# Down projection of an encoder trunk: one product of the next visit ahead of the last two of this one

## The chip, the cores and the metric

The kernel runs on one core of a Trainium2 chip, in one launch. The metric is the time of one execution on the device in microseconds (us). Three runs of the kernel before took 2561.51 to 2565.45 us, with a median of 2564.89 us. The engines are PE (TensorE: matrix products), DVE (VectorE), ACT (ScalarE), POOL (GpSimd), and SP, which only issues transfers here. Each engine works through its own list of instructions in order and waits at an instruction until its inputs are there.

## The reference

Two layers on 1024 tokens of width 1024, all in float32. The first mixes the tokens by attention and retention, the second by gated linear attention (GLA); each ends with a gated MLP whose gate goes through a convolution of width 3.

```python
for layer in range(2):
    if layer % 2 == 0:
        h = rmsnorm(x, mix_norm_even)
        x = x + concat(mla(...), retention(...)) @ w_out_even
    else:
        h = rmsnorm(x, mix_norm_odd)
        x = x + gla(...) @ w_out_odd
    h = rmsnorm(x, ffn_norm[layer])
    gate, val = split(h @ w_up[layer])            # 2 x 2816 columns
    gate = conv3(gate, conv_w[layer]) + conv_b[layer]
    x = x + (silu(gate) * val) @ w_down[layer]    # the down projection

# inside gla, for each of 4 heads (128 wide) and 2 directions:
log_a = log_sigmoid(ga @ w_gate + b_gate) / 16
b = cumsum(log_a)                                 # within a chunk
qc, kc = q * exp(b - b_mid), k * exp(b_mid - b)
out = mask(qc @ kc.T) @ v + (q * exp(b)) @ state
g = rmsnorm(out_fwd + out_bwd, out_norm) * silu(gr)
```

## The kernel before

Products in float32 are made of three passes: both operands are split into a high and a low part (`split`, L327: a cast on ACT at L329 and a subtraction on DVE or POOL at L330), and `mm3` (L348, its matmuls at L351) multiplies high by high, high by low and low by high.

The instructions are recorded in the order of the Python code, and a scheduler then orders each engine's list by its own estimate of who is ready. The order is fixed when the program is built. `act_set` (L145) asks for one instruction, the preload of a set of function tables on ACT (L146), to stay where the program put it.

**Tables on ACT.** A function such as Silu, Exp or Ln needs its set of tables to be the active one; where it is not, the built program has an `ACT_TABLE_LOAD` in front of the instruction. The set that is preloaded at L146, `natural_log_exp_and_others`, has Exp and Ln both. Without it, Exp and Ln each bring a set of their own. Silu (L1291, in the up projection) has another. The order of the kernel before has six loads: three at L146, two at L1291 and one at L257.

**Up projection.** `ffn` (L1133) makes 22 blocks of 128 columns of the gated product, each ended by `gated_mid` (L1279: convolution on DVE, Silu at L1291). `Mid` (L1298) writes the products to memory, the first 16 also as the differences that the down projection needs.

**Down projection** (`Down`, L1340). The first 16 blocks (`PAIRED`) are multiplied by a scheme of seven products in place of eight for a 2 x 2 block of the output. `VISITS` (L31) lists nine visits: the pair of output rows `m`, the first group of four blocks `g`, and one or two groups. The products of a visit are numbered 0 to 6 (A11, S2, A12, S3, S1, A22, S4, by the weight that they take) and add up in four banks: 0 and 2 in the first, 1 in the second, 3 and 5 in the third, 4 and 6 in the fourth. After each product DVE adds the bank to the output tile (L1437; the very first product of a pair is copied by ACT, L1435). So product 5 starts when DVE has added product 3, and between them on PE lies product 4 alone, and product 6 the same after 4.

Weights go through `weights` (L1380: four transfers a visit on SP, and two sums on POOL, L1389 and L1390), called when the first part of the visit ahead is due; `part` (L1394) splits one weight five products ahead of its use (`LEAD`), and after products 0 and 2 it asks POOL for the two other sums (L1406, L1408), which are written over a weight that has just been split or to a page of their own. The operands of a group come back from memory by `operands` (L1361). Six plain blocks follow (from L1487).

In the first layer `run` (L1449) asks for the preload of the Ln and Exp tables at L1453, since the norm and the GLA section that follow use them. In GLA the lines at stake are: the gates' Abs, Exp and Ln (L998 to L1000), the decays' Exp (L988), the output gates (L608, L609 and L611: Exp, Ln and Exp), the root of the norms by Ln and Exp (L359 to L361: Ln, Exp, Square), which DVE finishes at L363, and the copies L1021 and L1040. On PE they feed L854 (transposes), L1034 (states), L1104 (outputs, whose squares ACT sums at L1107) and L1119 (their transposes, after ACT has scaled them at L1113), woven between matmuls at L351 of the projections.

Of the kernel before, what the change touches and what calls it, by code (L numbers as in the profile page):

```python
# [10 lines left out]
F32 = mybir.dt.float32  # L11
# [3 lines left out]
ALU = mybir.AluOpType  # L15
AX = mybir.AxisListType

P = 128
# [4 lines left out]
H2 = 512  # L23
# [6 lines left out]
PAIRED, LEAD = 16, 5  # L30
VISITS = [(0, 0, 1), (2, 0, 2), (4, 0, 2), (6, 0, 2), (0, 1, 2), (2, 2, 2), (4, 2, 2), (6, 2, 2), (0, 3, 1)]  # L31
# [37 lines left out]
class Encoder:  # L69
# [1063 lines left out]
    def ffn(self, layer, h, ws, scale, h_gain, xs, gain=None, ahead=None):  # L1133
# [3 lines left out]
        nc = self.nc  # L1137
        mid = Mid(self)
        with ExitStack() as stack:
# [7 lines left out]
            with self.room("right", pp=2, wf=2):  # L1147
# [3 lines left out]
                r = scale()  # L1151
# [16 lines left out]
            with self.room("right", wf=6, sw=2):  # L1168
# [3 lines left out]
                for i, (g, then) in enumerate(zip(steps, steps[1:] + [None]), 3):  # L1172
                    next(g)
                    if then:
                        next(then)
                    else:
                        for p in range(1, 5):
                            down.operands(0, p)
                        down.begin()
                    for _ in g:  # L1180
                        pass
                    if i == PAIRED + 1:
# [157 lines left out]
class Down:  # L1340
# [8 lines left out]
    def __init__(self, e, layer, mid):  # L1349
        self.e, self.nc, self.mid = e, e.nc, mid  # L1350
        self.w = e.io["ffn_w_down"][layer].rearrange("(k p) f -> p k f", p=P)
        self.b, self.parts, self.raw, self.loads = {}, {}, {}, 0

    def stage(self, src):

# [24 lines left out]
    def weights(self, v):  # L1380

        e, nc, (m, g, n) = self.e, self.nc, VISITS[v]
        wg, wv = (e.page([P, 2, 2 * n, P], F32, "rb" if v % 2 else "raw") for _ in range(2))
        for x, c in ((wg, m), (wv, m + 1)):
            src = self.w[:, 4 * g:4 * (g + n), blk(c)].rearrange("p (j two) f -> p two j f", two=2)
            for i in range(2):
                nc.sync.dma_start(out=x[:, i], in_=src[:, i])
        s1, s4 = (e.page([P, 2 * n, P], tag="hx") for _ in range(2))
        nc.gpsimd.tensor_tensor(s1, wv[:, 0], wv[:, 1], ALU.add)  # L1389
        nc.gpsimd.tensor_tensor(wv[:, 0], wg[:, 0], wv[:, 0], ALU.subtract)  # L1390
        self.raw[v] = {self.A11: wg[:, 0], self.S2: wg[:, 0], self.A12: wg[:, 1], self.S3: wv[:, 0], self.S1: s1,
                       self.A22: wv[:, 1], self.S4: s4}

    def part(self, s):  # L1394

        if s >= 7 * len(VISITS):
            return
        e, nc, (v, p) = self.e, self.nc, divmod(s, 7)
# [5 lines left out]
        self.parts[s] = t  # L1404
# [10 lines left out]
    def product(self, s, ps, first):  # L1415
        t, (_, g, n) = self.parts.pop(s), VISITS[s // 7]
        bs = [b for i in range(n) for b in self.b[g + i, s % 7]]
        for j, b in enumerate(bs):
            self.e.mm3(ps, (t[:, 0, j], t[:, 1, j]), b, first and j == 0, j == 2 * n - 1, not first)

    def visit(self, v):
        e, nc, (m, g, n) = self.e, self.nc, VISITS[v]
        first, last = m not in self.u, g + n == PAIRED // 4
        if first:
            for i in range(2):
                for hf in range(2):
                    nc.sync.dma_start(out=self.x[m + i][hf], in_=self.xs[2 * (m + i) + hf])
            self.u[m] = e.page([P, H2], tag="hx")
        (c11, c12), (c21, c22), u = *self.x[m:m + 2], self.u[m]
        b1, b2, b3, b4 = (e.bank() for _ in range(4))  # L1430
        for p, (ps, x) in enumerate(((b1, u), (b2, u), (b1, c11), (b3, c22), (b4, c22), (b3, c21), (b4, c12))):
            s = 7 * v + p
            self.product(s, ps, p in (0, 1, 3, 4))
            if first and p == 0:
                nc.scalar.copy(x, ps)  # L1435
            else:
                nc.vector.tensor_tensor(x, ps, x, ALU.add)  # L1437
            self.part(s + LEAD)

            then = {0: 1, 3: 2, 4: 3}.get(v)  # L1440
            if then:
                self.operands(then, p)
            if v in (7, 8) and p in (1, 3, 4):
                self.rest({1: 0, 3: 1, 4: 2}[p] + 3 * (v - 7), {1: 2, 3: 3, 4: 1}[p])
        if last:
            for x in (c21, c12, c22):
                nc.gpsimd.tensor_tensor(x, x, u, ALU.add)

    def run(self, xs, gain, ahead, stack, ends):  # L1449
        e, nc, io = self.e, self.nc, self.e.io  # L1450
        self.xs, self.u = xs, {}
        if gain is not None:
            e.act_set(LN_EXP)  # L1453
            e.x_rooms()
# [248 lines left out]
```

## Time and profile before

| | |
|---|---|
| median of three runs | 2564.89 us (2561.51 to 2565.45) |
| the profiled execution | 2564.21 us |
| its span on the core | 2562.0 us |
| mean granted clock of PE over the span | 0.996 |
| down projection of layer 0 | 1166.1 to 1334.0 us |
| down projection of layer 1 | 2314.3 to 2484.1 us |
| GLA section | from about 1450 to 1808 us |

The prediction's rows come from one execution. A row of the timeline gives the start of an instruction (or of several alike, as x12), its duration, engine, line, operation, what it writes and reads, the form, and in brackets how long the engine had been idle before it and who released it. A clock of 1.00 is 2.4 GHz on PE, and 0.50 is 1.2 GHz.

### The profile page before, as it was taken

To read this page: it belongs to the slowest core of one execution; us is meant where nothing else is said; L and a number is where in the kernel's file an instruction comes from. 1 tells how busy PE (TensorE), PEld (TensorE's weight loads), DVE (VectorE), ACT (ScalarE), POOL (GpSimd) and SP (SyncE) were. 2 spreads that over 40 slices of the span, in tenths; PEclk is the share of its full clock that TensorE was granted. 3 is DMA by queue.
4 is the path that set the end of the run, shared out by engine and by line. 5 is a ranking of instruction groups with operands and counts; after the bars stand their busy time and mean duration, and the time that the engine had idled before them with its cause. 6 is when DMAs were issued, how large, how long until landed. Compare 5 with 4: busy or idle time off the path is not lost.

```text
span 2562.0 us, 33330 instructions
## 1 busy us (share of the span) xinstructions
PE 2501.4 (98%) x12584; PEld 2091.9 (82%) x12584; DVE 1811.6 (71%) x2855; ACT 1209.5 (47%) x2229; POOL 273.0 (11%) x286
## 2 busy tenths in 40 slices
PE   8999999999999999999999999999999999998999
PEld 8989877777888888887788898897788888886787
DVE  6545887878578877778767545648578777778762
ACT  5233767778444333334434445657443333334432
POOL 0000033443000000003230000000000000003330
PEclk9999999999999999999999999999999999999999
DMA  6111100003622332437524211223732332437523
GB/s 195 40 46 42 51 26 5 14 18 124 206 91 87 107 114 94 131 102 246 165 68 144 58 54 44 77 66 112 254 92 89 107 99 97 131 105 247 160 64 121
DMA packets 305813, 262.20 MB, mean 102 GB/s; under 512 B 15916, under 2 KB 240277, under 8 KB 305653
## 3 DMA queue, kind: packets, MB, share of 16 engines
q1 hardware_dynamic: 301045, 251.69, 31.1%
q10 hardware_dynamic: 4608, 8.39, 0.9%
q8 instruction: 99, 1.62, 0.3%
q14 instruction: 61, 0.50, 0.1%
HBM read 189.52 MB, written 70.52 MB: 101 GB/s over the span
## 4 chain that ended last, share of the span: by engine, by line
PE 67%; DVE 17%; DMA 6%; ACT 6%; issue 3%; POOL 1%; SPq 0%; DVEq 0%; ACTq 0%; POOLq 0%
PE mm L351 57%; DMA raw<-in_ffn_w_up 3%; DVE pg L1290 2%; ACT w L329 2%; DVE w L330 2%; DVE hx L1260 1%; PE mr L1104 1%; PE mr L351 1%; DMA pg<-d 1%; PE mr L1542 1%; DVE pg L1294 1%; DVE hx L330 1%; PE mr L1597 1%; PE mr L1544 1%; DVE h L330 1%
## 5 line engine op out<-in xcount | busy, mean ns | idle before, releaser
L351 PE MATMUL mm<-hx,w 128*128 128x512 f32 (+1 forms) x3408 | 828.9, 394 | 7.1 <-DVE w L330 2.5
L351 PEld LDWEIGHTS mm<-hx,w 128*128 128x128 f32 (+1 forms) x3408 | 635.9, 188 | 145.0 <-DVE w L330 3.4
L351 PE MATMUL mm<-h,w 128*128 128x512 f32 x1800 | 433.7, 394 | 14.4 <-DVE xt L1437 6.1
L351 PEld LDWEIGHTS mm<-h,w 128*128 128x128 f32 x1800 | 339.0, 190 | 90.2 <-DVE xt L1437 5.3
L329 ACT CAST w<-raw 128x1024 fp32r<-128x1024 f32 (+3 forms) x307 | 244.5, 802 | 354.6 <-PE mm L351 207.2
L330 DVE TENSOR_TENSOR w<-raw,w 128x1024 fp32r<-128x1024 f32 (+3 forms) x257 | 262.3, 1024 | 176.1 <-ACT w L329 159.8
L351 PE MATMUL mm<-w,hx 128*128 128x256 f32 (+1 forms) x2304 | 364.4, 306 | 2.4 <-POOL w L330 1.8
L351 PE MATMUL mm<-h,wf 128*128 128x512 f32 x1368 | 329.5, 390 | 2.6 <-DVE hx L1260 2.5
L351 PEld LDWEIGHTS mm<-w,hx 128*128 128x128 f32 x2304 | 308.0, 192 | 21.4 <-POOL w L330 2.8
L351 PEld LDWEIGHTS mm<-h,wf 128*128 128x128 f32 x1368 | 256.4, 188 | 58.1 <-DVE hx L1260 4.1
L1389 POOL TENSOR_TENSOR hx<-raw 128x512 f32<-128x512 f32 (+1 forms) x10 | 12.4, 1238 | 1545.4 <-ACT pg L1285 962.5
L329 ACT CAST wf<-raw 128x1024 fp32r<-128x1024 f32 x78 | 82.1, 1053 | 177.1 <-DVE raw L1246 133.1
L1260 DVE TENSOR_TENSOR hx<-mm,hx 128x512 f32<-128x512 f32 x190 | 130.2, 685 | 46.6 <-PE mm L351 46.6
L351 PE MATMUL mm<-hx,wf 128*128 128x512 f32 x552 | 132.4, 390 | 0.0
L351 PEld LDWEIGHTS mm<-hx,wf 128*128 128x128 f32 x552 | 103.4, 188 | 22.5 <-DVE hx L1260 1.1
L330 DVE TENSOR_TENSOR wf<-raw,wf 128x1024 fp32r<-128x1024 f32 x78 | 95.5, 1224 | 17.9 <-ACT wf L329 17.9
L351 PE MATMUL mm<-hr,hr 128*128 128x512 f32 x336 | 104.2, 404 | 1.4 <-ACT hf L1626 1.4
L1291 ACT ACTIVATE pg<-pg 128x1024 f32<-128x1024 f32 x44 | 46.7, 1062 | 122.7 <-DVE pg L1290 122.7
L1290 DVE SCALAR_TENSOR_TENSOR pg<-mm,c,pg 128x512 f32<-128x512 f32 (+1 forms) x100 | 73.7, 748 | 29.2 <-ACT pg L1285 29.2
L351 PE MATMUL mm<-hf,w 128*128 128x512 f32 x384 | 88.9, 392 | 0.0
L351 PEld LDWEIGHTS mm<-hf,w 128*128 128x128 f32 x384 | 72.2, 188 | 16.0
L330 POOL TENSOR_TENSOR w<-raw,w 128x512 fp32r<-128x512 f32 (+1 forms) x50 | 69.6, 1391 | 138.6 <-ACT w L329 94.0
(385 smaller groups left out, 3393.2 us busy)
## 6 DMA issues: line engine op xcount, KB each, us to landing
raw<-in_ffn_w_up SPq DMA_DIRECT2D x88, 512.0 KB
pg<-d SPq DMA_DIRECT2D x52, 512.0 KB
d<-tt SPq DMA_DIRECT2D x64, 256.0 KB
d<-pg SPq DMA_DIRECT2D x55, 256.0 KB
raw<-in_ffn_w_down SPq DMA_DIRECT2D x32, 384.0 KB
raw<-in_w_in_odd SPq DMA_DIRECT2D x24, 512.0 KB
raw<-in_w_out_even SPq DMA_DIRECT2D x16, 512.0 KB
st<-d SPq DMA_DIRECT2D x16, 512.0 KB
```

Source lines behind the costliest of these rows:

```text
L329: self.nc.scalar.copy(hi, src)
L330: return (rest or self.nc.vector).tensor_tensor(lo, src, hi.bitcast(F32), ALU.subtract)
L351: mm = lambda w, x, start, stop: self.nc.tensor.matmul(out, lhsT=w, rhs=x, start=start, stop=stop, skip_group_check=more)
L1104: nc.tensor.matmul(ps, lhsT=w[:, blk(t % 4)], rhs=x, start=n == 0, stop=n == len(terms) - 1)
L1260: add = lambda out, x, y: nc.vector.tensor_tensor(out, x, y, ALU.add)
L1290: nc.vector.scalar_tensor_tensor(dst, g[hf][:, src], cw(tap), dst, ALU.mult, ALU.add)
L1291: nc.scalar.activation(cv, cv, AF.Silu)
L1294: nc.vector.tensor_tensor(cv[:, sl], cv[:, sl], v[hf], ALU.mult)
L1389: nc.gpsimd.tensor_tensor(s1, wv[:, 0], wv[:, 1], ALU.add)
L1542: nc.tensor.matmul(ps[:, :192], lhsT=e.cq[k][hf][:, blk(t % 4)], rhs=w1[:, k], start=k == 0, stop=k == 2)
L1544: nc.tensor.matmul(ps[:, 256:], lhsT=e.ckv[k][hf][:, blk(t % 4)], rhs=w2[:, k], start=k == 0, stop=k == 1)
L1597: nc.tensor.matmul(ps, lhsT=qs.tok(0, t)[0], rhs=ks.hi[0][hf], start=True, stop=True)
```

## The change

The products of all visits are put in one list, `seq`: after products 1 to 4 of a visit comes product 0 of the next, and then products 5 and 6 of the first. `slot(k)` does the k-th of the list, `part(k)` its weight, five places ahead. The transfers of a visit's weights move to a place after the last split of the visit two before it, and its first two sums and the S2 sum (L1398 of the new kernel, on a page of its own) to a place after the split of the S3 weight of the visit before. S4 takes the page of A12. Product 0 of the first visit is recorded ahead of the rest of the last block of the up projection, and `begin` ahead of the operands of products 1 to 4.

```diff
                     else:
+                        down.begin()
                         for p in range(1, 5):
                             down.operands(0, p)
-                        down.begin()
+                        down.slot(0)
...
+        n = len(VISITS)
+        self.seq = [(0, 0)] + [x for v in range(n) for x in [(v, p) for p in range(1, 5)] + [(v + 1, 0), (v, 5), (v, 6)] if x[0] < n]
...
-        s1, s4 = (e.page([P, 2 * n, P], tag="hx") for _ in range(2))
+
+    def sums(self, v):
+        e, nc, (wg, wv) = self.e, self.nc, self.raw[v]
+        s1, s2 = (e.page([P, 2 * VISITS[v][2], P], tag="hx") for _ in range(2))
         nc.gpsimd.tensor_tensor(s1, wv[:, 0], wv[:, 1], ALU.add)
+        nc.gpsimd.tensor_tensor(s2, s1, wg[:, 0], ALU.subtract)
         nc.gpsimd.tensor_tensor(wv[:, 0], wg[:, 0], wv[:, 0], ALU.subtract)
-        self.raw[v] = {self.A11: wg[:, 0], self.S2: wg[:, 0], self.A12: wg[:, 1], self.S3: wv[:, 0], self.S1: s1,
-                       self.A22: wv[:, 1], self.S4: s4}
+        self.raw[v] = {self.A11: wg[:, 0], self.S2: s2, self.A12: wg[:, 1], self.S3: wv[:, 0], self.S1: s1,
+                       self.A22: wv[:, 1], self.S4: wg[:, 1]}
...
-        if not p and v + 1 < len(VISITS):
-            self.weights(v + 1)
...
-        if p == self.A11:
-            nc.gpsimd.tensor_tensor(r[p], r[self.S1], r[p], ALU.subtract)
         if p == self.A12:
             nc.gpsimd.tensor_tensor(r[self.S4], r[p], r[self.S2], ALU.subtract)
+        if p == self.S3 and v + 1 < len(VISITS):
+            self.sums(v + 1)
+        if p == self.S4 and v + 2 < len(VISITS):
+            self.weights(v + 2)
...
     def begin(self):
         self.weights(0)
-        for s in range(LEAD):
-            self.part(s)
+        self.weights(1)
+        self.sums(0)
+        for k in range(LEAD):
+            self.part(k)
...
+    def slot(self, k):
+        e, nc, (v, p) = self.e, self.nc, self.seq[k]
+        m, g, n = VISITS[v]
+        if not p:
+            self.ps[v] = [e.bank() for _ in range(4)]
...
+        if p == 1 and v < 4:
             for i in range(2):
                 for hf in range(2):
                     nc.sync.dma_start(out=self.x[m + i][hf], in_=self.xs[2 * (m + i) + hf])
...
+        self.part(k + LEAD)
...
     def run(self, xs, gain, ahead, stack, ends):
...
-        for v in range(len(VISITS)):
-            self.visit(v)
+        for k in range(1, len(self.seq)):
+            self.slot(k)
```

What the scheduler makes of it stands in the order of the built programs. First PE, at the end of a visit in the middle of layer 0's down projection, before (mm_11263 is the fourth bank, with product 4; mm_11262 the third, with product 5):

```order
L351 MATMUL mm_11263<-h_11083,w_11252 128x512
L351 MATMUL mm_11263<-h_11082,w_11252 128x512
L351 MATMUL mm_11262<-h_10939,w_11277 128x512
L351 MATMUL mm_11262<-h_10940,w_11277 128x512
...
L351 MATMUL mm_11262<-h_11098,w_11277 128x512
L351 MATMUL mm_11263<-hx_10945,w_11293 128x512
...
```

and of the changed kernel (mm_11222 and mm_11221 are the fourth and third banks, mm_11352 the first bank of the next visit):

```order
L351 MATMUL mm_11222<-h_11079,w_11258 128x512
L351 MATMUL mm_11222<-h_11078,w_11258 128x512
L351 MATMUL mm_11352<-hx_10775,w_11274 128x512
L351 MATMUL mm_11352<-hx_10776,w_11274 128x512
...
L351 MATMUL mm_11352<-hx_10919,w_11274 128x512
L351 MATMUL mm_11221<-h_10965,w_11294 128x512
L351 MATMUL mm_11221<-h_10966,w_11294 128x512
...
L351 MATMUL mm_11221<-h_11120,w_11294 128x512
L351 MATMUL mm_11222<-hx_10971,w_11310 128x512
```

Twelve matmuls of the next visit's product 0 now stand between products 4 and 5.

Second ACT, where layer 0's up projection ends, before (pg is the last block, L1291 its Silu, L146 the preload of the Ln and Exp tables):

```order
L329 CAST w_11013<-hx_10869 128x256
L329 CAST w_11039<-rb_10872 128x512
L329 CAST hx_10947<-pg_10943 128x512
L1291 ACTIVATE pg_10925<-pg_10925 128x1024
L146 ACT_TABLE_LOAD
L1435 COPY hx_10981<-mm_10982 128x512
```

and of the changed kernel, where the Silu stands at L1292 and the convolution's start at L1286:

```order
L1286 ACTIVATE pg_10951<-hx_10719,c_70 128x512
L146 ACT_TABLE_LOAD
L329 CAST w_11030<-raw_10834 128x256
L329 CAST w_11056<-hx_10865 128x512
L329 CAST w_11072<-rb_10840 128x512
L329 CAST w_11100<-rb_10841 128x512
L1292 ACT_TABLE_LOAD
L1292 ACTIVATE pg_10951<-pg_10951 128x1024
```

The preload stood behind the last Silu and now stands ahead of it, and the Silu has a load of its own. In the whole order of ACT the loads go from 6 to 95. Of the 89 more, one is this Silu's, and 88 stand from the norm after this down projection to the norm of the next MLP, in front of Ln (L359, L609, L1000) and of Exp (L360, L608, L611, L988, L999): 8 in the two norms, and 16, 18, 18 and 28 in the four heads of GLA.

Third ACT, in the part of GLA where head 1 starts (hf is an output gate, hr a gate of the decay), before:

```order
L608 ACTIVATE hf_14056<-hf_14056 128x512
L609 ACTIVATE hf_14056<-hf_14056 128x512
L998 ACTIVATE hr_14086<-mr_14085,c_70 128x512
L999 ACTIVATE hr_14086<-hr_14086 128x512
L611 ACTIVATE hf_14056<-hf_14056 128x512
L1000 ACTIVATE hr_14086<-hr_14086 128x512
L998 ACTIVATE hr_14102<-mr_14101,c_70 128x512
L999 ACTIVATE hr_14102<-hr_14102 128x512
L1000 ACTIVATE hr_14102<-hr_14102 128x512
```

and of the changed kernel:

```order
L608 ACTIVATE hf_14056<-hf_14056 128x512
L609 ACT_TABLE_LOAD
L609 ACTIVATE hf_14056<-hf_14056 128x512
L998 ACTIVATE hr_14086<-mr_14085,c_70 128x512
L999 ACT_TABLE_LOAD
L999 ACTIVATE hr_14086<-hr_14086 128x512
L611 ACTIVATE hf_14056<-hf_14056 128x512
L1000 ACT_TABLE_LOAD
L1000 ACTIVATE hr_14086<-hr_14086 128x512
L998 ACTIVATE hr_14102<-mr_14101,c_70 128x512
L999 ACT_TABLE_LOAD
L999 ACTIVATE hr_14102<-hr_14102 128x512
```

The activations stand in the same order as before, and between them are loads, ten from L609 here to the copy L1021 that ends this part (four of the ten in the rows shown).

## Rows read from the trace of the kernel before

**Rows 1.** The page's first part: busy time and share of the span by engine

```profile
PE 2501.4 (98%) x12584; PEld 2091.9 (82%) x12584; DVE 1811.6 (71%) x2855; ACT 1209.5 (47%) x2229; POOL 273.0 (11%) x286
```

**Rows 2.** Windows: layer 0's down projection, and its start; last columns clock, DMA share, GB/s

```profile
core 0: us, PE busy (x) PEld busy (x) DVE busy (x) ACT busy (x) POOL busy (x), PEclk, DMA share, GB/s
1166.00:1334.00 168.00, 158.84 (x679) 128.71 (x678) 124.22 (x164) 69.69 (x106) 59.11 (x40) 0.98 0.50 162
1170.00:1210.00 40.00, 35.65 (x146) 27.94 (x145) 35.74 (x47) 20.94 (x33) 13.50 (x8) 0.96 0.89 290
```

**Rows 3.** Waits in the two down projections: total us, times, longest

```profile
PE mm L351 <- DVE xa L1437: 4.8, 3, 2.3
PE mm L351 <- DVE w L330: 4.4, 4, 2.2
...
PE mm L351 <- DVE xt L1437: 6.1, 4, 2.2
```

**Rows 4.** Timeline of PE: start us, us, ..., [idle before, releaser]

```profile
1224.62 2.88 PE L351 MATMUL mm<-h,w 128*128 128x512 f32 x12
...
1237.58 3.02 PE L351 MATMUL mm<-h,w 128*128 128x512 f32 x12 [1.92 <-DVE xa L1437]
...
1259.21 4.54 PE L351 MATMUL mm<-h,w 128*128 128x512 f32 x12 [2.29 <-DVE xa L1437]
...
2386.23 4.60 PE L351 MATMUL mm<-h,w 128*128 128x512 f32 x12 [1.93 <-DVE xt L1437]
...
2409.31 4.39 PE L351 MATMUL mm<-h,w 128*128 128x512 f32 x12 [2.15 <-DVE xt L1437]
```

**Rows 5.** Timeline of DVE ahead of that wait

```profile
1257.25 1.21 DVE L330 TENSOR_TENSOR h<-pg,h 128x1024 fp32r<-128x1024 f32 x1
1258.38 0.68 DVE L1437 TENSOR_TENSOR xa<-mm,xa 128x512 f32<-128x512 f32 x1
```

**Rows 6.** Window of one slow stretch of PE's clock

```profile
1260.27:1263.68 3.41, 3.41 (x10) 2.63 (x9) 2.86 (x4) 1.04 (x1) 0.00 (x0) 0.50 0.79 242
```

**Rows 7.** Timeline of ACT at the last Silu of layer 0

```profile
1172.23 1.06 ACT L1291 ACTIVATE pg<-pg 128x1024 f32<-128x1024 f32 x1 [0.50 <-DVE pg L1290]
1173.31 1.28 ACT L146 ACT_TABLE_LOAD   x1
1174.60 0.59 ACT L1435 COPY hx<-mm 128x512 f32<-128x512 f32 x1
```

**Rows 8.** Window of the GLA section

```profile
1450.00:1808.00 358.00, 352.56 (x2054) 306.22 (x2053) 218.30 (x362) 212.58 (x455) 0.00 (x0) 1.00 0.24 74
```

**Rows 9.** Instruction groups of ACT there: busy us, mean ns, idle before, releaser

```profile
L988 ACT ACTIVATE hr<-hr 128x512 f32<-128x512 f32 (+1 forms) x96 | 49.8, 554 | 14.8 <-DVE hr L1010 14.5
...
L1107 ACT ACTIVATE hr<-mr 128x256 f32<-128x256 f32 x32 | 11.9, 378 | 35.7 <-PE mr L1104 35.7
```

**Rows 10.** Timeline of ACT, start of GLA's head 1

```profile
1546.22 0.63 ACT L609 ACTIVATE hf<-hf 128x512 f32<-128x512 f32 x1
...
1553.12 0.61 ACT L988 ACTIVATE hr<-hr 128x512 f32<-128x512 f32 x1
...
1557.71 0.21 ACT L988 ACTIVATE sr<-hr 128x4 f32<-128x4 f32 x1 [1.56 <-DVE hr L1004]
1557.83 0.57 ACT L1021 COPY hr<-mr 128x512 f32<-128x512 f32 x1
```

**Rows 11.** Timeline of all engines there: DVE's and PE's rows

```profile
1554.60 0.69 DVE L1018 TENSOR_TENSOR hr<-hr,hf 128x512 f32<-128x512 f32 x1
...
1555.34 0.66 PE L854 MATMUL mr<-c,hr 128*128 128x128 f32 x4 [0.57 <-DVE hr L1018]
...
1558.45 0.91 PE L1034 MATMUL mr<-hf,hr 128*128 128x256 f32 x3
```

**Rows 12.** Timeline of all engines at an output norm of head 0

```profile
1541.32 1.57 ACT L1113 ACTIVATE hr<-mr,sr 128x256 f32<-128x256 f32 x4 [0.46 <-DVE sr L363]
1543.71 1.03 PE L1119 MATMUL mr<-c,hr 128*128 128x128 f32 x8
```

More of the change, by code (lines that the diff above doesn't have):

```diff
@@ L1351, in __init__ @@
         self.w = e.io["ffn_w_down"][layer].rearrange("(k p) f -> p k f", p=P)
-        self.b, self.parts, self.raw, self.loads = {}, {}, {}, 0
+        self.b, self.parts, self.raw, self.loads, self.u, self.ps = {}, {}, {}, 0, {}, {}
+        n = len(VISITS)
+        self.seq = [(0, 0)] + [x for v in range(n) for x in [(v, p) for p in range(1, 5)] + [(v + 1, 0), (v, 5), (v, 6)] if x[0] < n]
     def stage(self, src):
@@ L1382, in weights @@
         e, nc, (m, g, n) = self.e, self.nc, VISITS[v]
-        wg, wv = (e.page([P, 2, 2 * n, P], F32, "rb" if v % 2 else "raw") for _ in range(2))
-        for x, c in ((wg, m), (wv, m + 1)):
+        self.raw[v] = [e.page([P, 2, 2 * n, P], F32, "rb" if v % 2 else "raw") for _ in range(2)]
+        for x, c in zip(self.raw[v], (m, m + 1)):
             src = self.w[:, 4 * g:4 * (g + n), blk(c)].rearrange("p (j two) f -> p two j f", two=2)
@@ L1387, in weights, with part @@
                 nc.sync.dma_start(out=x[:, i], in_=src[:, i])
-        s1, s4 = (e.page([P, 2 * n, P], tag="hx") for _ in range(2))
+    def sums(self, v):
+        e, nc, (wg, wv) = self.e, self.nc, self.raw[v]
+        s1, s2 = (e.page([P, 2 * VISITS[v][2], P], tag="hx") for _ in range(2))
         nc.gpsimd.tensor_tensor(s1, wv[:, 0], wv[:, 1], ALU.add)
+        nc.gpsimd.tensor_tensor(s2, s1, wg[:, 0], ALU.subtract)
         nc.gpsimd.tensor_tensor(wv[:, 0], wg[:, 0], wv[:, 0], ALU.subtract)
-        self.raw[v] = {self.A11: wg[:, 0], self.S2: wg[:, 0], self.A12: wg[:, 1], self.S3: wv[:, 0], self.S1: s1,
-                       self.A22: wv[:, 1], self.S4: s4}
-    def part(self, s):
-        if s >= 7 * len(VISITS):
+        self.raw[v] = {self.A11: wg[:, 0], self.S2: s2, self.A12: wg[:, 1], self.S3: wv[:, 0], self.S1: s1,
+                       self.A22: wv[:, 1], self.S4: wg[:, 1]}
+    def part(self, k):
+        if k >= len(self.seq):
             return
-        e, nc, (v, p) = self.e, self.nc, divmod(s, 7)
-        if not p and v + 1 < len(VISITS):
-            self.weights(v + 1)
+        e, nc, (v, p) = self.e, self.nc, self.seq[k]
         r = self.raw[v]
@@ L1403, in part @@
         e.split(r[p], t[:, 0], t[:, 1])
-        self.parts[s] = t
-        if p == self.A11:
-            nc.gpsimd.tensor_tensor(r[p], r[self.S1], r[p], ALU.subtract)
+        self.parts[v, p] = t
         if p == self.A12:
             nc.gpsimd.tensor_tensor(r[self.S4], r[p], r[self.S2], ALU.subtract)
+        if p == self.S3 and v + 1 < len(VISITS):
+            self.sums(v + 1)
+        if p == self.S4 and v + 2 < len(VISITS):
+            self.weights(v + 2)
     def begin(self):
         self.weights(0)
-        for s in range(LEAD):
-            self.part(s)
[L1415 to L1423, printed above, removed]
+        self.weights(1)
[3 more added lines that the diff above has]
+    def slot(self, k):
+        e, nc, (v, p) = self.e, self.nc, self.seq[k]
+        m, g, n = VISITS[v]
+        if not p:
+            self.ps[v] = [e.bank() for _ in range(4)]
+        first = m not in self.u
         if first:
+            self.u[m] = e.page([P, H2], tag="hx")
+        if p == 1 and v < 4:
             for i in range(2):
@@ L1427, in visit @@
                     nc.sync.dma_start(out=self.x[m + i][hf], in_=self.xs[2 * (m + i) + hf])
[L1428 to L1447, printed above, removed]
+        ps, start = self.ps[v][(0, 1, 0, 2, 3, 2, 3)[p]], p in (0, 1, 3, 4)
+        t = self.parts.pop((v, p))
+        bs = [b for i in range(n) for b in self.b[g + i, p]]
+        for j, b in enumerate(bs):
+            e.mm3(ps, (t[:, 0, j], t[:, 1, j]), b, start and j == 0, j == 2 * n - 1, not start)
+        if first:
+            nc.scalar.copy(self.u[m], ps)
+        else:
+            x = self.u[m] if p < 2 else self.x[m + (p in (3, 4, 5))][p in (3, 4, 6)]
+            nc.vector.tensor_tensor(x, ps, x, ALU.add)
+        self.part(k + LEAD)
+        then = {0: 1, 3: 2, 4: 3}.get(v)
+        if then:
+            self.operands(then, p)
+        if v in (7, 8) and p in (1, 3, 4):
+            self.rest({1: 0, 3: 1, 4: 2}[p] + 3 * (v - 7), {1: 2, 3: 3, 4: 1}[p])
+        if p == 6 and g + n == PAIRED // 4:
+            for x in (self.x[m + 1][0], self.x[m][1], self.x[m + 1][1]):
+                nc.gpsimd.tensor_tensor(x, x, self.u[m], ALU.add)
     def run(self, xs, gain, ahead, stack, ends):
         e, nc, io = self.e, self.nc, self.e.io
-        self.xs, self.u = xs, {}
+        self.xs = xs
         if gain is not None:
```

## The prediction, made before the changed kernel ran

> **What bounds the kernel now.** I read the busy shares first: PE works 2501.4 of the 2562.0 us, so only what keeps PE waiting, or slows its clock, counts [rows 1]. Next the windows of the part that the change names: 158.84 us busy of 168.00 in layer 0's down projection, and the first 40 us, where PE is busy 35.65 and DVE 35.74 [rows 2]. The waits say which release is last: at the start the weights' splits on DVE (4.4 us in 4 waits), and later the additions of a bank (4.8 us in 3 waits in layer 0, 6.1 in 4 in layer 1) [rows 3]. The timeline shows the place: a product's twelve matmuls take 2.88 us undisturbed, and ahead of product 5 PE waits up to 2.3 us for the addition of product 3 [rows 4]. DVE was at a split of 1.21 us when the addition at 1258.38 became ready [rows 5]; product 4 alone, 2.9 us, doesn't cover that. Of the four waits of 1.9 us or more, three are followed by a product of 4.39 to 4.60 us instead of 2.88 [rows 4]: behind the idle PE the granted clock is 0.50, the lower of the two levels, for 3.41 us [rows 6]. That costs half of 3.41, 1.7 us.
>
> Then I read the order of ACT far behind the changed lines, because the preload moves there. In GLA ACT is busy 212.58 of 358.00 us and PE 352.56 [rows 8]: PE bounds, ACT has 145 us of air.
>
> **The change, part by part.** The sum starts from the profiled execution, 2564.21 us (span 2562.0 and 2.2 around it), 0.7 below the median of the runs; I count from 2564.2.
>
> *Products interleaved.* No matmul is added or taken away. Product 5 now stands two products behind 3, so DVE has some 5.6 us for the addition instead of 2.9, and the longest wait was 2.3: the waits on additions go, 4.8 in layer 0 and in layer 1 6.1 less one at the start of 0.8, 5.3. With them go the three slow stretches, one in layer 0 and two in layer 1: 5.1. That is 15.2. What is late next is the split of the weights, whose lead stays five products; DVE has 124 of 168 us there [rows 2], so it keeps up after the start. Lower bound: the waits move to the splits and nothing is gained; upper bound: the start's waits go too, 4.4 more in layer 0 and as much in layer 1, 24.
>
> *Sums ahead, own page for S2, weights two visits ahead.* POOL has the same four sums a visit, 59 us of 168, with ACT and DVE waiting for PE rather than for it. On SP four transfers a visit go earlier, and the output tiles' four from product 0 to product 1; the DMA engines have half their time free over the stretch (0.50), but in the first 40 us 0.89 is taken [rows 2], and the second visit's weights now ask for their share there. PE's rows name no transfer as the last release. I cost it at nothing after the start; cover gone, a late weight would cost one product of 2.9 us.
>
> *Start.* Product 0 of the first visit ahead of the up projection's last matmuls gives DVE one product of room, 2.7 us, where it is busy 36 of 40 us. It gains between 0 and 4.4 a layer, or loses a late weight's 2.9; I take 1.5, so 3, since DVE's work there stays the same. Together 18.2 (-3 to 24).
>
> *Preload ahead of the last Silu.* The Silu now loads its own tables and nothing brings Ln and Exp back together, so 88 more loads stand in the norms and the heads of GLA. One load: the Silu ended at 1173.29, the copy behind the load began at 1174.60, so 1.31 us for a recorded 1.28 [rows 7]; between activations that overlapped before, by 0.09 as at 1557.71 and 1557.83 [rows 10], 1.40. I take 1.33. All 88 are 117 us of ACT. What of it reaches PE is worked out at two places.
>
> First, the start of head 1. Ten loads stand from the Exp-Ln gate at 1546.22 to the copy L1021 at 1557.83 [rows 10]; 13.3 us. ACT had one gap in it, 1.56 us before 1557.71, and PE's L1034 starts at 1558.45, 0.05 behind the copy's end at 1558.40 [rows 10, 11]. So PE is late there by 13.3 - 1.56 - 0.05 = 11.7. (A part of it comes sooner: six loads stand ahead of the Exp at 1553.12; its end goes from 1553.73 to 1561.7, DVE's L1018 from 1554.60 by 7.2, and PE's L854, which has waited 0.57 for it already, with it.) PE's list offers nothing else meanwhile, because the order is fixed.
>
> Second, an output norm: four loads (gate twice, Ln, Exp) stand ahead of L1113, which ends at 1542.89; PE's L1119 starts at 1543.71 [rows 12]. 5.3 - 0.8 = 4.5.
>
> That makes 16.2 for 14 loads. The head's other four stand by twos before shorter queues; I take half price, 2.7. Head 1: 18.9 for its 18 loads, 1.05 each. At that price the 80 loads of the four heads cost 84. For the eight in the two norms, which stand where ACT serves a whole row of casts, I take a third, 0.3 each: 2.5. Bounds: below, nothing if all fits in ACT's air; above, all 88 at 1.33, 117.
>
> New waits of over 1.9 us bring slow stretches: three of four had one [rows 4]. I count some three such waits a head, twelve, and with one behind seven of them, since later ones may fall on lateness already paid: 7 at 1.7 are 12. Bounds 0 and 20.
>
> The Trainium skill ("ScalarE: Activation LUTs", What ACT_TABLE_LOAD costs) puts a switch at 1283 ns of load, which the row agrees with, and some 1380 ns of drain on top, 2.66 us together. The trace of before shows 0.02 us ahead of the load and 0.01 behind it, so not that drain. By the page my estimate of a load that reaches PE would be 1.38 us higher, and the sum some 110 us.
>
> Sum: 2564.2 - 18.2 + 84 + 2.5 + 12 = 2644.5; I say 2644.
>
> **The rivals.**
>
> *Half the lateness is caught up (2595).* While PE waits, ACT works on, and idle time ahead of the next chain could swallow lateness. For: ACT idles 35.7 us before L1107 and 14.8 before L988 [rows 9]. Against: before L1107 it waits for PE's own outputs, so that gap comes again after every delay, and the loads that follow it hit at once. Half of 84, 1 and 6 against 18.2: 2564.2 + 30.8 = 2595.
>
> *The loads cost nothing, and the kernel is faster (2546).* One mechanism, ACT's air in GLA: 145 us idle against 117 of loads. It decides for this if each consumer of ACT has slack for the one to ten loads ahead of it, more than 13 us at the head's start. Against: the consumer there had 0.05 [rows 10, 11]. The same time comes out if the loads aren't executed as ordered. 2564.2 - 18.2.
>
> *The interleaving brings nothing (2663).* DVE at 36 of 40 us at the start, with the DMA engines at 0.89 [rows 2], goes on bounding, the waits pass from additions to splits, and only the loads show. For: the start's waits are the splits' [rows 3]. Against: after the start DVE has a quarter of its time free. 2564.2 + 98.5.
>
> *A switch costs more than its record (2753).* If a load that reaches PE takes as long again, each costs PE 1.05 + 1.33 and the heads' 84 turn into 190, the norms' 2.5 into 5: 2564.2 - 18.2 + 190 + 5 + 12. Nothing in the rows shows such a time [rows 7]; only loads with another set's function next to them on both sides could, and before has few.
>
> **How the numbers follow.** My sum has 0.70, the rival of half 0.13, the interleaving without gain 0.10, the free loads 0.04, the dearer switch 0.03. All but the free loads are slower, 0.96; of it I take 0.02 for the end of the rival of half at which the hidden share is so large that gain and loss cancel. A change under 0.2%, 5 us, is what a measurement of this kernel can't tell from none. Faster 0.04, same 0.02, slower 0.94. The range holds my sum with its unknown parts (gain 8 to 24, heads 65 to 105, norms 0 to 5, clock 0 to 20: some 2605 to 2686) and reaches to the rival of half below and past the one without gain above: 2590 to 2685.
>
> **What would show it right or wrong.** In the profile of the changed kernel: no waits of PE on L1437's successor in the down projections, and layer 1's down projection, where no preload is involved, 8 to 12 us shorter; 95 table loads on ACT of 1.28 us; GLA's stretch some 85 to 100 us longer than its 358, with PE waiting for DVE L1018, ACT L1021 and ACT L1113 by several us each (renumbered by a few lines at most), and a clock under 1.00 there. It is wrong if ACT's loads show but PE's waits don't grow by them (then the air hides them), if the loads are followed by pauses of a microsecond (then a switch costs more), or if the down projections still wait for additions or, in their place, for weights.

## The result, and the profile after

The changed kernel takes 2651.3 us (median of 4 runs, 2645.7 to 2656.9) against 2564.0: slower, by a ratio of 1.034 with an interval of 1.031 to 1.037. The forecast was 2644, in a range of 2590 to 2685. The execution whose trace is read here took 2656.9 us, 5.6 above the median.

The page's first part, which answers [rows 1]:

```profile
PE 2533.2 (95%) x12584; PEld 2112.9 (80%) x12584; DVE 1806.9 (68%) x2855; ACT 1325.8 (50%) x2318; POOL 267.7 (10%) x286
```

ACT has 116 us more, which is 89 loads of 1.28 and little else. PE does the same 12584 matmuls in 32 us more, and is idle longer. Where, the window between the same two matmuls of GLA shows, which answers [rows 8] (columns as in [rows 2]):

```profile
1450.60:1902.40 451.80, 384.61 (x2054) 325.00 (x2053) 222.05 (x362) 317.63 (x535) 0.00 (x0) 0.92 0.19 59
```

The stretch grew from 358.0 to 451.8 us. Of the 93.8, PE's idle time has 61.8 (from 5.4 to 67.2) and its busy time 32.0, at a clock of 0.92 instead of 1.00. Whom PE waits for there (total us, times, longest):

```profile
PE mr L854 <- DVE hr L1018: 24.5, 5, 7.1
PE mr L1119 <- ACT hr L1113: 19.2, 8, 4.3
PE mr L1034 <- ACT hr L1021: 14.7, 6, 5.2
PE mr L1104 <- DVE hr L1094: 4.6, 4, 1.3
```

and before, in the window of [rows 8]:

```profile
PE mr L854 <- DVE hr L1018: 3.7, 6, 0.8
PE mr L1119 <- ACT hr L1113: 1.0, 2, 0.8
PE mr L1034 <- ACT hr L1021: 0.2, 1, 0.2
```

These three are the consumers that the prediction had worked out. The timeline of ACT at the start of head 1 answers [rows 10]:

```profile
1574.38 0.63 ACT L999 ACTIVATE hr<-hr 128x512 f32<-128x512 f32 x1
1575.03 1.28 ACT L1000 ACT_TABLE_LOAD   x1
1576.32 0.63 ACT L1000 ACTIVATE hr<-hr 128x512 f32<-128x512 f32 x1
...
1588.52 0.21 ACT L988 ACTIVATE sr<-hr 128x4 f32<-128x4 f32 x1
1588.63 0.57 ACT L1021 COPY hr<-mr 128x512 f32<-128x512 f32 x1
```

and that of PE answers [rows 11, 12]:

```profile
1561.89 2.42 PE L1119 MATMUL mr<-c,hr 128*128 128x128 f32 x8 [3.21 <-ACT hr L1113]
...
1572.36 3.58 PE L351 MATMUL mm<-hx,w 128*128 128x512 f32 x15
1581.48 1.11 PE L854 MATMUL mr<-c,hr 128*128 128x128 f32 x4 [5.54 <-DVE hr L1018]
1582.25 4.08 PE L351 MATMUL mm<-hx,w 128*128 128x512 f32 x11
1589.25 3.35 PE L1034 MATMUL mr<-hf,hr 128*128 128x256 f32 x7 [2.92 <-ACT hr L1021]
```

A load starts 0.02 us behind the activation before it, and the next activation 0.01 behind the load: 1.31 a switch, and no drain. The gap of 1.56 us that ACT had before L988 is gone. Eleven matmuls that took 2.76 us take 4.08 behind the wait, at the lower clock, and L1034 waits 2.92 all the same. Before, they were

```profile
1555.75 2.76 PE L351 MATMUL mm<-hx,w 128*128 128x512 f32 x11
```

In the down projections PE's waits in the changed kernel are these, first layer 0, then layer 1:

```profile
PE mm L351 <- ACT h L329: 4.7, 2, 2.8
PE mm L351 <- DVE xa L1448: 2.0, 1, 2.0
...
PE mm L351 <- ACT w L329: 4.1, 1, 4.1
PE mm L351 <- ACT h L329: 2.4, 1, 2.4
PE mm L351 <- DVE xt L1448: 1.1, 1, 1.1
```

L1448 is the addition (L1437 before). Both waits for it lie at the starts; past them one wait is left in each layer, 1.90 and 2.38 us for the cast of an operand (h).

Traces can be laid side by side by the same matmuls. In us, by the position in PE's list:

| stretch (its start before) | before | changed | order_only | set_later | own_s4 | before_no_preload |
|---|---|---|---|---|---|---|
| down projection of layer 0, start (1160) | 39.8 | 41.5 | 39.7 | 39.2 | 42.5 | 40.0 |
| its rest (1200) | 134.1 | 129.0 | 127.0 | 131.4 | 126.7 | 136.1 |
| norm and first projections (1334) | 117.8 | 121.7 | 117.8 | 117.8 | 117.8 | 121.6 |
| GLA, first quarter (1452) | 86.0 | 100.2 | 86.0 | 86.0 | 86.0 | 100.2 |
| second (1538) | 88.1 | 109.9 | 88.1 | 88.1 | 88.1 | 109.9 |
| third (1626) | 89.0 | 109.9 | 89.0 | 89.1 | 89.0 | 109.9 |
| fourth (1715 to 1810) | 95.0 | 132.0 | 94.5 | 94.5 | 94.0 | 131.6 |
| MLP of layer 1 (1897) | 402.8 | 407.0 | 402.3 | 402.8 | 402.3 | 404.0 |
| its down projection, start (2300) | 50.0 | 50.8 | 48.6 | 48.8 | 51.4 | 49.9 |
| its rest (2350 to 2484) | 134.1 | 127.3 | 124.8 | 126.9 | 124.7 | 133.3 |

So the changed kernel loses 93.9 us in GLA, 3.9 in the norm and 4.2 in the next MLP, and gains 9.4 in the two down projections. Each column is one execution, and that limits what a row of a down projection can tell. In layer 1's, four kernels run the same instructions (changed, set_later, and preload_head2 and filler below): their starts take 50.8, 48.8, 48.5 and 48.9 us, their rests 127.3, 126.9, 129.2 and 129.6. In layer 0's, where set_later differs, the other three take 41.5, 43.1 and 42.0, and 129.0, 131.4 and 131.8. So a difference of less than some 3 us between two traces there isn't shown.

### The profile page after: what moved, and what is told of

Its sections match the earlier page's. It is cut to its first block, busy times and chain, and to the rows that moved or that the text cites. A ratio compares the mean times of both kernels' runs of the same rounds, so it can differ in the third digit from the quotient of the medians.

```text
span 2655.1 us, 33429 instructions
## 1 busy us (share of the span) xinstructions
PE 2533.2 (95%) x12584; PEld 2112.9 (80%) x12584; DVE 1806.9 (68%) x2855; ACT 1325.8 (50%) x2318; POOL 267.7 (10%) x286
## 5 line engine op out<-in xcount | busy, mean ns | idle before, releaser
L351 PE MATMUL mm<-hx,w 128*128 128x512 f32 (+1 forms) x3408 | 843.9, 398 | 10.6 <-ACT h L329 4.3
L351 PEld LDWEIGHTS mm<-hx,w 128*128 128x128 f32 (+1 forms) x3408 | 645.4, 191 | 151.8 <-ACT w L329 5.1
L330 DVE TENSOR_TENSOR w<-raw,w 128x1024 fp32r<-128x1024 f32 (+3 forms) x257 | 259.1, 1010 | 177.1 <-ACT w L329 163.2
L329 ACT CAST wf<-raw 128x1024 fp32r<-128x1024 f32 x78 | 82.1, 1052 | 189.6 <-DVE raw L1247 134.1
L330 DVE TENSOR_TENSOR wf<-raw,wf 128x1024 fp32r<-128x1024 f32 x78 | 95.5, 1224 | 21.1 <-ACT wf L329 21.0
L1292 ACT ACTIVATE pg<-pg 128x1024 f32<-128x1024 f32 x44 | 46.7, 1062 | 121.2 <-DVE pg L1291 121.2
L1291 DVE SCALAR_TENSOR_TENSOR pg<-mm,c,pg 128x512 f32<-128x512 f32 (+1 forms) x100 | 73.6, 746 | 29.5 <-ACT pg L1286 29.5
L330 POOL TENSOR_TENSOR w<-raw,w 128x512 fp32r<-128x512 f32 (+1 forms) x50 | 67.9, 1358 | 141.7 <-ACT w L329 99.4
```

Of the source, the lines that this page charges most:

```text
L329: self.nc.scalar.copy(hi, src)
L330: return (rest or self.nc.vector).tensor_tensor(lo, src, hi.bitcast(F32), ALU.subtract)
L351: mm = lambda w, x, start, stop: self.nc.tensor.matmul(out, lhsT=w, rhs=x, start=start, stop=stop, skip_group_check=more)
L1291: nc.vector.scalar_tensor_tensor(dst, g[hf][:, src], cw(tap), dst, ALU.mult, ALU.add)
L1292: nc.scalar.activation(cv, cv, AF.Silu)
```

## The experiments

**set_later.** The changed kernel, with the preload asked for fourteen products later.

```diff
-            e.act_set(LN_EXP)
...
             self.slot(k)
+            if k == 14 and gain is not None:
+                e.act_set(LN_EXP)
```

> The changed kernel with one edit: the preload of the Ln and Exp set is asked for fourteen products later, so that it stands behind the last Silu again; ACT's order has 6 loads instead of 95. Theory (the 88 loads in the norms and in GLA are the loss, and the interleaving gains what the two down projections show in the changed kernel's trace, 4.0 and 3.5 us): 2564 - 7.5 = 2556, between 2552 and 2560, GLA's stretch back at 358 us with its clock at 1.00. Rival A (the interleaving itself disturbs GLA, by its buffers or transfers, and the loads lie in idle time): over 2620. Rival B (the down projection's gain is the 18.2 of the sum, and the profiled execution of the changed kernel was a bad one): 2546.

It takes 2551.5 us (2549.9 to 2553.3), 0.995 of before, with an interval of 0.994 to 0.996: 99.8 less than the changed kernel. The window of GLA, from 1450 to 1808 us, is that of [rows 8]:

```profile
1450.00:1808.00 358.00, 352.99 (x2041) 305.71 (x2040) 219.53 (x363) 213.73 (x455) 0.00 (x0) 1.00 0.25 76
```

Rival A falls. The time lies half way between the theory's 2556 and rival B's 2546, and 0.5 below the theory's range.

**before_no_preload.** The kernel before, without the line `e.act_set(LN_EXP)` in the down projection.

> The kernel before with one edit: the preload of the Ln and Exp set in the down projection of layer 0 is left out, so that ACT's order has 93 loads, the 88 of the changed kernel among them; the products stand as before. Theory (the loads alone are the loss): 2564 + 94 for GLA + 0 to 4 for the norms = 2660, between 2653 and 2668, with PE's idle time in GLA up by some 62 us and the slow clock by some 34. Rival A (the interleaving is needed for the loss): 2562 to 2580. Rival C (the waits of the norms, 3.8 us, come from the changed start of the norm and not from loads): 2656.

It takes 2664.6 us, a ratio of 1.039 with an interval of 1.037 to 1.040, so 100.8 longer than before. Its window of GLA reads as that of the changed kernel:

```profile
1458.20:1909.40 451.20, 384.76 (x2054) 325.25 (x2053) 222.06 (x362) 317.83 (x535) 0.00 (x0) 0.93 0.19 59
```

The loads are enough for the loss without anything of the interleaving, and by the table the norm's 3.8 come with them: rivals A and C fall.

**preload_head2.** The changed kernel, with the set brought back at head 2.

```diff
             for hd in range(4):
+                if hd == 2:
+                    self.act_set(LN_EXP)
```

> The changed kernel, with the preload of the Ln and Exp set asked for once more where GLA's head 2 begins: 40 of the 88 loads stay (the first norm, heads 0 and 1, three at the start of head 2), 48 go. Theory (each head pays for its own loads and nothing is carried on or made up later; in the changed kernel's trace the first norm lost 3.8, heads 0 and 1 lost 14.2 and 21.8): 2551.5 + 39.8 + 2 to 4 for the start of head 2 = 2594, between 2588 and 2600, heads 2 and 3 back at 89.5 and 141 us. Rival A (lateness is made up in the later heads, where ACT has air again): 2565 to 2582. Rival B (the loss hangs on something else than the loads): over 2630.

It takes 2602.3 us (1.015, interval 1.014 to 1.017), 8 more than expected and 2 above the range. From the preload to the end of GLA PE's waits are those of before again, where they were 1.5 in two and 1.0 in two (total us, times, longest; renumbered by two):

```profile
PE mr L854 <- DVE hr L1020: 1.5, 2, 0.8
PE mr L1121 <- ACT hr L1115: 0.9, 2, 0.7
```

Nothing is made up there, so rival A falls; nothing more is lost either. The expectation had left out head 1's second output norm, which stands in the third quarter: the lateness grew there by 5.0 us in the changed kernel, and this quarter by 9.5 here. The start of the down projection, 43.1 against 39.2 in set_later, adds 3.9, while the norm and the first two quarters together lose 37.1, less than the 39.8 expected.

**order_only.** The later preload, and of the change the order of the products alone: sums and pages of a visit as before. A visit's transfers are asked for at the split of the S1 weight of the visit before it, not of its A11 weight, but start at like times: those of the seventh visit at 1232.4 us, 1238.2 before.

```diff
-        s1, s2 = (e.page([P, 2 * VISITS[v][2], P], tag="hx") for _ in range(2))
+        s1, s4 = (e.page([P, 2 * n, P], tag="hx") for _ in range(2))
...
+        if p == self.S1 and v + 1 < len(VISITS):
+            self.weights(v + 1)
...
+        if p == self.A11:
+            nc.gpsimd.tensor_tensor(r[p], r[self.S1], r[p], ALU.subtract)
```

> The kernel with the later preload, where only the order of the products is new: weights, their sums and pages are as in the kernel before (transfers one visit ahead, S2 over A11 after its split, S4 on its own page). Theory (the waits for the additions are removed by the order alone, 10.1 us and three slow stretches of 1.7; the sums were not on the path): 2564 - 12 = 2552, between 2548 and 2557. Rival (the order needs the sums early, since S2's sum waits for A11's split and now has one product less): 2560 to 2566, with PE waiting for a weight's split ahead of product 1.

It takes 2543.9 us (0.993, interval 0.991 to 0.994), 7.6 less than set_later, and 4 below the range of the theory, which had counted on 12 us and not on 20. Past the start, PE waits for nothing in either down projection; its only waits in layer 0 are

```profile
PE mm L351 <- DVE xa L1441: 5.1, 2, 3.4
```

So the order gains 20 us, and the rest of the change gives 7.6 of them back. By the table 6.5 of these lie in the rests of the down projections (131.4 and 126.9 against 127.0 and 124.8), none at the starts. The size comes from one trace each, but the sign repeats: the four kernels with S4 on A12's page and the new order (changed, set_later, preload_head2, filler) have rests of 129.0 to 131.8 and 126.9 to 129.6, the five with the new order and S4 on its own page 126.7 to 127.3 and 124.7 to 124.8.

**own_s4.** set_later, and S4 on a page of its own.

```diff
-        s1, s2 = (... for _ in range(2))
+        s1, s2, s4 = (... for _ in range(3))
...
-                       self.A22: wv[:, 1], self.S4: wg[:, 1]}
+                       self.A22: wv[:, 1], self.S4: s4}
```

> The kernel with the later preload, and S4 gets a page of its own again instead of A12's, so that POOL's order has the S4 sum ahead of the next visit's sums in each visit. Theory (in the changed kernel S4 must wait for A12's split, so POOL does the next visit's sums first, which wait 15 to 18 us for their transfer; ACT's cast of S4, and the casts of operands behind it, wait with it, and PE for 2.8 + 0.8 and 1.9 us in layer 0 and 2.4 in layer 1): 4 to 8 us below the later preload alone, so 2549 if that is 2556, and ACT's longest wait for L1413 under 2 us. Rival (those casts wait for their own transfers from memory): the same as the later preload within 2 us, with the waits of PE still there.

It takes 2549.6 us (0.994, interval 0.993 to 0.996), 1.9 less than set_later, which the intervals don't keep apart, and less than the 4 to 8 expected. In the traces the place is plain. In the changed kernel, all engines:

```profile
1260.77 1.29 POOL L1397 TENSOR_TENSOR hx<-raw 128x512 f32<-128x512 f32 x1 [18.40 <-DMA raw<-in_ffn_w_down]
...
1264.64 1.29 POOL L1413 TENSOR_TENSOR rb<-rb,hx 128x512 f32<-128x512 f32 x1
1265.96 0.62 ACT L329 CAST hx<-st 128x512 fp32r<-128x512 f32 x1 [10.19 <-POOL rb L1413]
...
1268.57 1.62 PE L351 MATMUL mm<-hx,w 128*128 128x512 f32 x6 [1.90 <-ACT h L329]
```

POOL stands for 18.40 us at the next visit's first sum, whose weight is still on its way; the S4 sum of this visit is behind it, ACT's queue behind that, and PE comes to wait for the cast of an operand (h), which has nothing to do with S4. With a page of its own POOL's order has S4 first:

```profile
1249.49 1.53 POOL L1413 TENSOR_TENSOR hx<-rb,hx 128x512 f32<-128x512 f32 x1 [11.16 <-issue]
1253.73 1.39 POOL L1397 TENSOR_TENSOR hx<-raw 128x512 f32<-128x512 f32 x1 [2.71 <-DMA raw<-in_ffn_w_down]
```

and the rests take 126.7 and 124.7 us, as with the order alone. But the starts are longer than those of set_later by 3.3 and 2.6 us, so in these traces most of the gain is lost there; by the spread given above that isn't shown to be more than chance.

The page does more than order POOL's sums. A visit's weights land in pages of the visit two before it, and SP waits for the splits that read these (DVE w L330). With S4 on A12's page that is the last split of a visit. The seventh visit's transfers start, before, in the changed kernel (both pairs) and in own_s4:

```profile
1238.18 0.93 SPq L1387 DMA_DIRECT2D raw<-in_ffn_w_down  x2
...
1252.27 0.93 SPq L1391 DMA_DIRECT2D raw<-in_ffn_w_down  x2
1254.57 0.92 SPq L1391 DMA_DIRECT2D raw<-in_ffn_w_down  x2
...
1238.94 0.93 SPq L1391 DMA_DIRECT2D raw<-in_ffn_w_down  x2
```

So the changed kernel issues them some 14 us later than before, though the change was to bring them earlier, and this is the weight that POOL stands 18.40 us for.

**s2_page.** order_only, and S2 on a page of its own, asked for when it was.

```diff
-        s1, s4 = (... for _ in range(2))
+        s1, s2, s4 = (... for _ in range(3))
...
-            nc.gpsimd.tensor_tensor(r[p], r[self.S1], r[p], ALU.subtract)
+            nc.gpsimd.tensor_tensor(r[self.S2], r[self.S1], r[p], ALU.subtract)
```

> The kernel with the order alone (2543.9) and one edit: S2 has a page of its own instead of standing over A11; when the sums are asked for stays as it was. Theory (a third hx page per visit delays the operands' pages, transfers and casts at the start of each down projection): 2547 to 2551. Rival (the time at which sums and weights are asked for decides, not the page): 2542 to 2546.

It takes 2545.8 us (0.993, interval 0.992 to 0.994), inside the range of the rival, and the intervals don't keep it apart from order_only. The starts are 41.8 and 50.4 us, 2.1 and 1.8 longer than with the order alone, and there PE now waits for the cast of a weight (layer 0):

```profile
PE mm L351 <- ACT w L329: 4.6, 2, 3.2
```

PE is idle there for 5.2 and 5.3 us, with the order alone for 5.2 and 4.7; most of the difference is the clock, whose mean is 0.92 and 0.93 in place of 0.96. Like own_s4 it has three hx pages a visit where the order alone and set_later have two, but weights_two, with two, has starts of 39.5 and 50.7. That a third page makes the starts longer is not shown.

**weights_two.** order_only, with each visit's transfers and its S1 and S3 sums two visits ahead, asked for where the changed kernel asks for the transfers.

```diff
-        if p == self.S1 and v + 1 < len(VISITS):
-            self.weights(v + 1)
...
+        if p == self.S4 and v + 2 < len(VISITS):
+            self.weights(v + 2)
...
         self.weights(0)
+        self.weights(1)
```

> The kernel with the order alone (2543.9) and one edit: a visit's transfers, with the S1 and S3 sums, are asked for two visits ahead instead of one. Theory of the pages: 2543 to 2548, since S1 and S4 hold their hx pages longer, but no third one is taken. Rival (transfers two visits ahead take the DMA engines from the operands in the first 40 us): 2549 to 2556, with PE's waits at the start for ACT's casts of operands.

It takes 2542.7 us (0.993, interval 0.991 to 0.994): no cost. But the transfers start no sooner for it, those of the seventh visit at 1233.1 us against 1232.4 in order_only, so the run shows that asking for them sooner costs nothing, and not what sooner transfers would do.

**sums_only.** set_later, with the products in the old order.

```diff
-        self.seq = ... [(v, p) for p in range(1, 5)] + [(v + 1, 0), (v, 5), (v, 6)] ...
+        self.seq = ... [(v, p) for p in range(1, 7)] + [(v + 1, 0)] ...
```

> The later preload, and everything of the change but the order of the products: they stand 0 to 6 within a visit again, with the weights two visits ahead, the sums three products ahead and S4 on A12's page. The order alone measured 2543.9 and the whole with the later preload 2551.5, so the rest costs 7.6 beside the order. Theory (that cost belongs to the earlier sums and weights and to their pages, whatever the order): 2563.8 + 7.6 = 2571, between 2567 and 2576, with the waits of 1.9 to 2.3 us for additions still there. Rival (the cost arises from the two together; alone, the early sums take waits off the splits): 2558 to 2564.

It takes 2561.0 us (0.999, interval 0.998 to 1.000), the same as before and in the rival's range, so the theory of a cost in any order falls. In the trace, of an execution of 2565.2 us and so 4 above the median, two things cancel: the starts take 43.5 and 51.7 us instead of 39.8 and 50.0, with one wait for a split of

```profile
PE mm L351 <- DVE w L330: 5.5, 1, 5.5
```

and the rests 131.8 and 130.2 instead of 134.1. It has two hx pages a visit, so a third one isn't the only thing that can make a start longer.

**filler.** The changed kernel with useless matmuls on PE ahead of L854.

```diff
+            ps = self.bank()
+            if d and hf:
+                for _ in range(16):
+                    nc.tensor.matmul(ps, lhsT=self.wg[d][:96, blk(hd)], rhs=self.ga[hf][:96], start=True, stop=True)
```

> The changed kernel (2651.3) with useless work on PE: in each head of GLA sixteen matmuls of 96x512, about 3.6 us, stand in the order of PE right ahead of the first transposes L854, where PE waits 4.3 to 7.1 us for DVE L1018. Their output is overwritten by the transposes. Theory 1 (ACT's lateness sets the time; the slow clock behind the waits only takes the place of waiting): the fillers fit into the waits, and the time stays at 2651, between 2646 and 2655. Theory 2 (the slow stretches come on top of the waits, 34 us of them in GLA): the fillers keep PE busy, some of the stretches behind L854 vanish, 1.7 to 3.4 us a head: 2638 to 2645. Theory 3 (the waits at L854 aren't for ACT, but PE itself is late): 4 x 3.6 longer, 2666.

It takes 2670.5 us (1.042, interval 1.041 to 1.044), near the 2666 of theory 3, but not for its reason. The timeline of PE at head 1:

```profile
1574.35 1.57 PE L351 MATMUL mm<-hx,w 128*128 128x512 f32 x6
1575.75 3.81 PE L1024 MATMUL mr<-c,c 96*128 96x512 f32 x16
1584.41 1.11 PE L1026 MATMUL mr<-c,hr 128*128 128x128 f32 x4 [4.84 <-DVE hr L1018]
```

Where fifteen matmuls of the projection stood ahead of the wait, six stand now and the fillers: the scheduler has put the others later, and the wait is still 4.84 us. What the fillers do alone shows at the start of head 0, where nothing was late yet, first in the changed kernel and then here:

```profile
1469.98 1.11 PE L854 MATMUL mr<-c,hr 128*128 128x128 f32 x4 [4.33 <-DVE hr L1018]
1476.74 3.78 PE L1034 MATMUL mr<-hf,hr 128*128 128x256 f32 x8 [2.24 <-ACT hr L1021]
...
1469.85 1.11 PE L1026 MATMUL mr<-c,hr 128*128 128x128 f32 x4 [1.81 <-DVE hr L1018]
1478.65 2.08 PE L1040 MATMUL mr<-hf,hr 128*128 128x256 f32 x4 [5.26 <-ACT hr L1027]
```

The transposes start when they did, with some 2.5 us more of matmuls ahead of them (the fillers' 3.8, less five useful ones that moved behind). So they wait for ACT and DVE, and theory 3 falls at this place. The states behind them start 1.9 us later, because the order of ACT is another too: an Exp with its load (L988, at 1476.10) now stands ahead of the copy L1027, which starts at 1478.03 instead of 1476.12. Against the changed kernel the same matmuls are soon 2.9 us late, and stay so to the end of the head. The run changes more than it was to change, and doesn't tell theories 1 and 2 apart.

**two_ahead.** order_only, with products 0 and 1 of the next visit ahead of 5 and 6.

```diff
-        ... [(v, p) for p in range(1, 5)] + [(v + 1, 0), (v, 5), (v, 6)] ...
+        ... [(v, p) for p in range(1 if not v else 2, 5)] + [(v + 1, 0), (v + 1, 1), (v, 5), (v, 6)] ...
```

> The kernel with the order alone (2543.9) and one edit: products 0 and 1 of the next visit stand ahead of products 5 and 6, so that three or four products lie between 3 and 5. Theory (what is left at the start of each down projection are waits for additions, 3.4 + 1.7 and 3.3 + 1.4 us, and a slow stretch of 1.7 behind the first): they go, 2531 to 2536. Rival (the start is bound by transfers and by DVE, which has the last block's convolution to do; the waits pass to a split or a cast of the products that now come sooner): 2541 to 2548.

It takes 2538.6 us (2536.7 to 2539.9; 0.990, interval 0.989 to 0.992), the lowest median of all, 24 us under before and 113 under the changed kernel. The time lies between the two expectations. The waits for additions are nearly gone, and a split of the operands has come in their place (layer 0):

```profile
PE mm L351 <- DVE h L330: 1.9, 1, 1.9
PE mm L351 <- ACT h L329: 0.6, 1, 0.6
PE mm L351 <- DVE xa L1441: 0.6, 2, 0.4
```

The starts take 36.9 and 46.1 us, the rests are unchanged: so both expectations were half right.

## Why the prediction was right, point by point

*The preload.* Right in mechanism and place: two kernels with the loads and two without show it from both sides. A load was priced at 1.33 and costs 1.31. At the start of head 1 the lateness was to grow by 11.7 us up to L1034; by the same matmuls it grew from 20.7 to 30.8. At the second output norm 4.5 were forecast and 3.4 came, and for two pairs of loads 2.7 against 3.3 together (1.8 and 1.6).

*Waits and clock.* The two terms of GLA were mis-sized and made up for one another. Forecast were 84 us of waits and 12 of slow clock; measured are 61.8 and 32. That 96 lies so near to 93.8 is luck. The step that failed is the count "three such waits a head, twelve, and with one behind seven of them, since later ones may fall on lateness already paid". There were thirteen waits of more than 1.9 us, but the clock was at 0.50 for 68 us, which is twenty stretches of 3.4 and not seven. A part of that replaces waiting, as the eleven matmuls at 1582.25 show, which stretched by 1.3 us into a wait, and a part comes on top, as behind L1034. How much is which was not settled, since filler changed the order of both engines.

*Norms.* 2.5 forecast; 3.9 in the norm behind the down projection. In the next one PE waits 1.46 us for the norm in each of the three traces with all 88 loads (changed, before_no_preload, filler), and not before. The rest of the 4.2 in the next MLP is no price of the loads: it is mostly a wait of 1.99 us at 2331.24, which is 0.3 or none in the other two, and the slow clock behind it. So 5.4 came, and the third of a price was too low.

*Interleaving.* 15.2 forecast past the start, and the order alone gained 7.1 + 9.3 = 16.4: right. In the changed kernel it was 5.1 + 6.8 = 11.9. Layer 1's down projection became 6.0 us shorter, not 8 to 12, and its waits for L1448 and for the cast of a weight (1.1 and 4.1 us, both at the start) are what the prediction had named as a sign of being wrong. What failed is the step "I cost it at nothing after the start": the sums and pages cost 7.6 us between set_later and order_only, and 6.5 of these lie in the rests, where S4 on A12's page keeps POOL, ACT and then PE waiting, as own_s4 shows by taking it away. Two premises of the step were wrong. "On SP four transfers a visit go earlier": in layer 0 they started 3 to 14 us later from the third visit on. And "ACT and DVE waiting for PE rather than for it" (POOL): in the trace of before ACT already waited for POOL in layer 0's down projection:

```profile
ACT w L329 <- POOL raw L1406: 13.6, 3, 5.4
ACT w L329 <- POOL rb L1406: 13.3, 3, 5.7
```

Of the starts, 3 us of gain were forecast; set_later has 0.6 and 1.2, and the changed kernel loses 1.7 and 0.8. In layer 1 nothing in the program differs, and the starts of the two other kernels that are the same there, 48.5 and 48.9, put it down to the execution. In layer 0 the Silu has its own load there, and the three kernels that have it take 41.5 to 43.1 against 39.2 in the one trace of set_later; that the load is the cause is not shown.

*The sum.* The trace, 5.6 us above the median, has 9.4 of gain for 18.2, a loss of 93.9 for 96 in GLA and of 8.1 for 2.5 in the norm and the next MLP. These make the 12 us by which it lies above the sum.

*Rivals.* Half caught up: preload_head2 shows no making up. Free loads and the dearer switch: excluded by set_later and before_no_preload, and by the gaps of 0.02 and 0.01 us. The Trainium skill's drain of some 1380 ns ("ScalarE: Activation LUTs", What ACT_TABLE_LOAD costs) shows in no row here, also where the loads stand between two functions that need them. Interleaving without gain: wrong, by order_only.

## What to carry to other kernels

Where a scheduler orders the engines' lists, look for what an edit moves far from its own lines: here an instruction without inputs slid ahead of the one that undoes it, and a gain of 12 us turned into a loss of 87. A preload that serves a later stage is safe only behind the last user of another table set, and the order of the built program shows it before any run. And a result that takes the page of an operand must wait until that is read; in a queue that runs in order, work that waits for a transfer can then stand ahead of it, and the transfer that takes the page next starts later, wherever the code asks for it.

## What the runs showed that was not expected

The clock took part of the place of waiting: PE at 0.50 for 68 of the 452 us in GLA, behind waits of 2.2 to 7.1 us, where before there was none. And matmuls put in front of a wait to fill it did not bring time: PE's list had 3.8 us of fillers there and the wait went from 5.54 to 4.84 only. Nine useful matmuls, 2.0 us, had moved behind it, and the matmuls between the output norm and the wait took 1.1 us less, at a higher clock. The wait ended 19.59 us behind the first transposes of that norm in both kernels (1561.89 to 1581.48, 1564.82 to 1584.41): so ACT and DVE, not PE, set that time.
